# The S5 scan of a hybrid encoder as two real scans in a turning frame, with reordered mixer steps

## The chip, the cores and the metric

The kernel runs on one core of a Trainium2 chip. What counts is the device time of one execution, in microseconds (us). Engines are named as the profile names them: PE is TensorE (PEld its weight loads), DVE is VectorE, ACT is ScalarE, POOL is GpSimd, SP is SyncE, which issues DMA transfers. "PEclk" is the clock that TensorE was granted, as a share of full speed.

## The reference

Two layers over x of 512 tokens by 1024 channels. Each layer projects x once, and gives the columns to three mixers: a bidirectional S5 (256 channels), a bidirectional gated linear attention in chunks of 64 (256 channels), and a windowed attention with rotary embedding (512 channels). Then follow the output projection with a layer norm, and a feed-forward part of width 4096 (squared ReLU) with another.

```
lam_bar = exp(lam * step)                       # complex, per group and state
bu = einsum('zgph,blgh->zblgp', b_bar, u)
h[t] = lam_bar * h[t-1] + bu[t]                 # forward; and the same backward
y = Re(c0 . h_f) + Re(c1 . h_b) + d * u ;  z = gelu(y) ;  y_A = val * sigmoid(gate)
x = LN(alpha*x + concat(y_A, y_B, y_C) @ w_out)
x = LN(alpha*x + relu(x @ w_ff1)**2 @ w_ff2)
```

## The kernel before

**Matmuls.** Each large product is taken as three (low by high, high by low, high by high; `mm3`, L251 to L254). A weight unit (`wunit`) is loaded by SP into `raw`, copied by ACT into WA (high half, L221), and its low half is the difference that DVE (sometimes POOL) makes (L248). The first of the three matmuls needs the low half.

**S5.** The 512 tokens of a group are 64 chunks of 8. `tb_params` makes, on DVE, the complex powers of lam_bar (`powers`). `tables(l)` makes from them the tables of one layer: the products L541 to L564, transposes on TensorE (tile `wst`, L568), the in-chunk kernel (tile `lag`, L576 to L582), and it writes them to scratch in HBM (`scr_st`, `scr_out`, and 15 transfers `scr_lag`, L588 and L590, on SP). `s5_states` gives the contribution of each chunk, `M.Vs`: real and imaginary part, 16 groups, 64 chunks on 128 partitions (64 states forward, 64 backward). `s5_scan` turns this into the state before each chunk, `M.H`. It takes two levels: inside blocks of 8 chunks a complex step for j = 1 to 7 (L761 to L764, four DVE instructions each); over the 8 block ends six complex steps on 128x32 (L772 to L775); and a third part that adds the power times the block's entry state (L785 to L793), whose second half, the imaginary parts, is on POOL in layer 0 and on DVE in layer 1 (`sc1`). `s5_out` multiplies M.H with the output tables.

**Linear attention.** `gla_gates` (decays, L613, L615, tile `gs`), `gla_scores` (q_in L636, k_in, scores `gsc` L645 on TensorE, masked copy L646 on DVE), `gla_states`, `gla_out` (statistics in GLS), `gla_y` (`goT` on TensorE).

**Windowed attention.** Rotary embedding L873 to L875, queries transposed as `qT` (L907), split at L914 and L915, then `swa`.

**Feed-forward.** For some block pairs `ff1_pair` (L1036 on) takes a Strassen form: two weight blocks r1 and r2 are loaded by SP (L1041, L1042) into the scratch tile MA, alternately in its columns 0 to 2047 and 2048 to 4095; DVE makes sums (L230), ACT copies each unit into WA and DVE makes its low half (L1060); the products are the 128x256 tiles `f1s`.

**Order.** The steps of a mixer are written in the order that the table `seq` gives for each layer (`u` and `st0`/`st1` are the S5 input and states, `g0`, `g2`, `g3` the other projections, `w0` to `w3` the windowed attention of each query block, `y` the end of the linear attention). A scheduler then places every instruction by that order as priority, so the queues interleave the steps. Layer 1's tables are written behind the first quarter of layer 0's first feed-forward matrix (`tables(1)`, released by a step named `ff3`), and so run under the feed-forward stage. Scratch tiles are shared: MA holds attention scratch in the mixer, tables in front of layer 1, and the blocks r1 and r2.

Of the kernel before, what the change touches and what calls it, by code (L numbers as in the profile page):

```python
# [64 lines left out]
def trunk(tc, I, out, dbg=None):  # L65
# [300 lines left out]
    def tb_params():  # L366
# [116 lines left out]
        V.tensor_scalar(AIS_[:, 0], APW_[:, 1, :, 0], -1.0, None, op0=MUL)
        V.tensor_copy(AIS_[:, 1], APW_[:, 1, :, 0])
        V.tensor_scalar(A8S_[:, 0], APW_[:, 1, :, 7], -1.0, None, op0=MUL)
        V.tensor_copy(A8S_[:, 1], APW_[:, 1, :, 7])

# [261 lines left out]
    def s5_scan(l):  # L749
        APW, AIS, A8S = [t[:, :, 16 * l:16 * l + 16] for t in (APW_, AIS_, A8S_)]  # L750
        DB("V", M.Vs.rearrange("p r g b j -> p (r g b j)"))
        DB("APW", APW_.rearrange("p a b c -> p (a b c)"))
# [6 lines left out]
        for j in range(1, 8):
            x = M.Vs[:, :, :, :, j - 1]  # L760
            V.tensor_tensor(T1, x, ar, op=MUL)  # L761
            V.tensor_tensor(T2, x[:, ::-1], ai, op=MUL)
            V.tensor_tensor(T1, T1, T2, op=ADD)
            V.tensor_tensor(M.Vs[:, :, :, :, j], M.Vs[:, :, :, :, j], T1, op=ADD)  # L764
        a8 = bc(APW[:, 0, :, 7], 1, 2)
        V.memset(EST[:, :, :, 0], 0.0)
        for b in range(7):
            if b == 0:
                V.tensor_copy(EST[:, :, :, 1], M.Vs[:, :, :, 0, 7])
                continue  # L770
            x = EST[:, :, :, b]
            V.tensor_tensor(ETM[:, 0], x, a8, op=MUL)  # L772
            V.tensor_tensor(ETM[:, 1], x[:, ::-1], A8S, op=MUL)
            V.tensor_tensor(ETM[:, 0], ETM[:, 0], ETM[:, 1], op=ADD)
            V.tensor_tensor(EST[:, :, :, b + 1], M.Vs[:, :, :, b, 7], ETM[:, 0], op=ADD)  # L775
# [2 lines left out]
        for r, eng, n, buf in ((0, V, 8, y2), (1, E("sc1", l), 4, TAB[:, 512:1024])):
            for i in range(16 // n):
                gs = slice(n * i, n * i + n)  # L780
                P1 = buf[:, 0:64 * n].rearrange("p (g b j) -> p g b j", g=n, b=8)
# [561 lines left out]
```

## Time and profile before

| | us |
|---|---|
| median of three runs | 1242.35 (1240.74 to 1243.05) |
| the profiled execution | 1247.4 |
| its span in the trace | 1245.6, granted clock 0.977 |
| PE busy | 1169.3 (94%) |
| DVE busy | 901.5 (72%) |
| ACT busy | 553.4 (44%) |
| POOL busy | 164.1 (13%) |

The profile describes the one execution of 1247.4 us. A busy share is an average over stages; a stage's own limit is read from a window of it, and from what the engine with the gap waited for. Sections of the run: layer 0's mixer lasts to about 280 us, the output projection and the feed-forward part to about 640, layer 1's mixer to about 910, the rest is layer 1's projection and feed-forward.

### The profile page before, as it was taken

What the parts mean: (1) busy time and instruction counts of PE and PEld (TensorE: products, weight loads), DVE (VectorE), ACT (ScalarE), POOL (GpSimd) and SP (SyncE); (2) the same over time, 40 slices, a digit from 0 to 9 for tenths busy, and PEclk for the clock granted to TensorE, in tenths of its full rate; (3) what the DMA queues carried; (4) which work ended last, traced back from release to release, by engine and by line L of the source; (5) the groups of instructions that cost most, each with busy time, mean ns of one, the idle gap of its engine ahead of it and who ended that gap; (6) DMA issues with size and microseconds to landing.
All of it is one profiled execution on the core that took longest, in us unless ns stands there. A gap on an engine that the chain in (4) does not pass through costs nothing.

```text
span 1245.6 us, 18803 instructions
## 1 busy us (share of the span) xinstructions
PE 1169.3 (94%) x7400; PEld 985.5 (79%) x7400; DVE 901.5 (72%) x1727; ACT 553.4 (44%) x937; POOL 164.1 (13%) x123
## 2 busy tenths in 40 slices
PE   6696978999999999999999989799999999999997
PEld 4684765678888889989987867556898898998986
DVE  8986988659875675758564399883987485764957
ACT  4253247534522543725533535572465272461640
POOL 3422352112000000000141020220400000000000
PEclk9898999999999999999999999899999999999999
DMA  6340431113453532412422414302144142250331
GB/s 219 103 153 9 73 123 52 52 34 105 123 166 143 159 104 68 150 54 69 153 82 74 158 34 66 122 17 85 35 138 150 51 142 79 88 164 20 100 121 68
DMA packets 50616, 121.68 MB, mean 98 GB/s; under 512 B 13280, under 2 KB 20320, under 8 KB 50528
## 3 DMA queue, kind: packets, MB, share of 16 engines
q1 hardware_dynamic: 37680, 103.53, 25.2%
q10 hardware_dynamic: 12848, 16.95, 5.3%
q8 instruction: 58, 0.95, 0.3%
q14 instruction: 30, 0.25, 0.1%
HBM read 110.53 MB, written 8.88 MB: 96 GB/s over the span
## 4 chain that ended last, share of the span: by engine, by line
PE 67%; DVE 9%; DMA 2%; ACT 2%; issue 1%; SPq 1%; ACTq 0%; DVEq 0%
PE o L252 11%; PE o L253 11%; PE o L254 11%; PE f1s L252 6%; PE f1s L254 6%; PE f1s L253 6%; PE so L968 2%; PE proj L253 1%; PE proj L254 1%; PE proj L252 1%; PE f1e L253 1%; PE pT L962 1%; PE f1e L254 1%; PE f1e L252 1%; DVE XR L319 1%
## 5 line engine op out<-in xcount | busy, mean ns | idle before, releaser
L221 ACT ACTIVATE WA<-raw 128x1024 fp32r<-128x1024 f32 (+2 forms) x129 | 132.4, 1029 | 140.7 <-DMA raw<-in_w_ff 39.2
L248 DVE TENSOR_TENSOR WA<-raw,WA 128x1024 fp32r<-128x1024 f32 (+1 forms) x102 | 121.8, 1195 | 89.8 <-ACT WA L221 89.8
L221 ACT ACTIVATE WA<-MA 128x1024 fp32r<-128x1024 f32 (+1 forms) x72 | 64.5, 913 | 138.4 <-PE o L254 102.2
L979 DVE SCALAR_TENSOR_TENSOR XR<-XR,o 128x512 f32<-128x512 f32 (+1 forms) x81 | 52.7, 676 | 90.4 <-PE o L254 90.3
L1060 DVE TENSOR_TENSOR WA<-MA,WA 128x1024 fp32r<-128x1024 f32 (+1 forms) x72 | 74.4, 1043 | 17.0 <-ACT WA L221 17.0
L252 PE MATMUL f1s<-xs,WA 128*128 128x256 f32 x288 | 81.6, 283 | 0.2 <-DVE MA L230 0.2
L254 PE MATMUL f1s<-xs,WA 128*128 128x256 f32 x288 | 81.5, 283 | 0.0
L253 PE MATMUL f1s<-xs,WA 128*128 128x256 f32 x288 | 81.5, 283 | 0.0
L248 POOL TENSOR_TENSOR WA<-raw,WA 128x1024 fp32r<-128x1024 f32 (+2 forms) x27 | 61.4, 2280 | 130.0 <-ACT WA L221 123.6
L230 POOL TENSOR_TENSOR XR<-XR,lt 128x512 f32<-128x512 f32 (+1 forms) x13 | 18.5, 1421 | 394.1 <-ACT XR L218 394.1
L230 DVE TENSOR_TENSOR MA<-MA,f1s 128x256 f32<-128x256 f32 x120 | 49.6, 418 | 28.6 <-PE f1s L254 19.6
L252 PE MATMUL o<-WA,yYa 128*128 128x512 f32 (+1 forms) x162 | 64.0, 395 | 0.8 <-DVE XR L979 0.7
L253 PE MATMUL o<-WA,yQ 128*128 128x512 f32 (+1 forms) x164 | 63.4, 386 | 0.0
L252 PE MATMUL o<-WA,yQ 128*128 128x512 f32 (+1 forms) x164 | 63.3, 386 | 0.0
L252 PE MATMUL o<-WA,yYb 128*128 128x512 f32 (+1 forms) x162 | 63.0, 389 | 0.0
L253 PE MATMUL o<-WA,yYa 128*128 128x512 f32 (+1 forms) x162 | 63.0, 389 | 0.0
L253 PE MATMUL o<-WA,yYb 128*128 128x512 f32 (+1 forms) x162 | 63.0, 389 | 0.0
L254 PE MATMUL o<-WA,yYb 128*128 128x512 f32 (+1 forms) x162 | 62.8, 389 | 0.0
L252 PE MATMUL o<-WA,yP 128*128 128x512 f32 x160 | 62.8, 392 | 0.0
L254 PE MATMUL o<-WA,yYa 128*128 128x512 f32 (+1 forms) x162 | 62.7, 387 | 0.0
L254 PE MATMUL o<-WA,yQ 128*128 128x512 f32 (+1 forms) x164 | 62.7, 385 | 0.0
L253 PE MATMUL o<-WA,yP 128*128 128x512 f32 x160 | 62.7, 392 | 0.0
(460 smaller groups left out, 3566.0 us busy)
## 6 DMA issues: line engine op xcount, KB each, us to landing
raw<-in_w_ff SPq DMA_DIRECT2D x80, 512.0 KB, 3.5
MA<-in_w_ff SPq DMA_DIRECT2D x48, 512.0 KB, 3.5
raw<-in_wg SPq DMA_DIRECT2D x23, 512.0 KB, 4.0
raw<-in_w_out SPq DMA_DIRECT2D x16, 512.0 KB, 3.9
scr_out<-MA SPq DMA_DIRECT2D x8, 512.0 KB, 3.7
yc<-scr_out ACTq DMA_DIRECT2D x8, 512.0 KB, 4.4
raw<-in_wg SPq DMA_DIRECT2D x8, 288.0 KB, 2.9
MA<-in_s5cb ACTq DMA_DIRECT2D x8, 256.0 KB, 4.2
```

The costliest lines, as they stand in the source:

```text
L221: S.activation(out=o_, in_=i_, func=AF.Copy)
L230: eng.tensor_tensor(o_, a, b, op=op)
L248: (eng or V).tensor_tensor(WA[:, i, 1, c], raw[:, c], WAf[:, i, 0, c], op=SUB)
L252: T.matmul(ps, a[1], b[0], start=first, stop=False)
L253: T.matmul(ps, a[0], b[1], start=False, stop=False)
L254: T.matmul(ps, a[0], b[0], start=False, stop=last)
L319: V.scalar_tensor_tensor(x[:, c], x[:, c], mean, M.lng[:, c], op0=SUB, op1=MUL)
L962: T.transpose(ps[:, b * 128:b * 128 + 128], P[:, h, b * 128:b * 128 + 128], ident)
L968: T.matmul(ps[64 * v:64 * v + 64, :], av[:, tt - 1 + b0 + b, 64 * v:64 * v + 64], M.pT[v][:, b].rearrange("p h q -> p (h q)"), start=(b == ...
L979: V.scalar_tensor_tensor(x, x, scale, ps, op0=MUL, op1=ADD)
L1060: V.tensor_tensor(WA[:, u, 1, c], src, WAf[:, u, 0, c], op=SUB)
```

## The change

`s5_scan` no longer works in blocks. With lam_bar to the 8th written as a real size times a turn, every chunk's contribution is turned back by its chunk number (cos and sin in the new table ROT, 128 x 2 x 16 x 64), so that what remains is a recurrence with a real factor. That is one `tensor_tensor_scan` for the real and one for the imaginary parts (128x1024 each, the factor in TAB, set to 0 at each group's first chunk). Then the result is turned forward again, with the last sum written into M.H. All of it is on DVE, except the copy of the factor into TAB on ACT.

`tb_params` no longer makes the powers 1 to 8 of lam_bar to the 8th (APW and its copies); it squares the size and the turn three times (MG8, RW) and corrects the turn's length (`unit_`). `turns(l)` makes ROT from RW by doubling, six rounds of four DVE instructions, in two scratch areas of MA (columns 0 to 2047). `turns(0)` is a new step in layer 0 behind the gates, `turns(1)` is written behind `tables(1)`. The order table `seq` changes in both layers; in layer 0, `scan` comes behind `out`, `g2` ahead of the scores, `y` behind `w3`.

```diff
-    "seq": ["u st0 g0 tb st1 gates scan scores states sink g2 out g3 y keys late s5o w0 w1 w2 w3", "u tb st0 st1 g0 gates scan scores sink g2 states out g3 y keys late s5o w0 w2 w1 w3"],
+    "seq": ["u g0 st0 tb st1 gates turns g2 scores states sink out scan g3 keys late w0 s5o w3 y w1 w2", "tb g0 u gates st0 st1 scan scores states sink g2 out g3 y keys late s5o w0 w2 w1 w3"],
...
-        V.tensor_copy(APW_[:, :, :, 0], PW[:, :, :, 8])
-        powers(APW_, -1)
...
+        for k in range(3):
+            V.tensor_tensor(MG8, mag if k == 0 else MG8, mag if k == 0 else MG8, op=MUL)
+        wc, ws = RW[:, 0], RW[:, 1]
+        for k in range(3):
+            V.scalar_tensor_tensor(u1, ws, 2.0, wc, op0=MUL, op1=MUL)
+            V.tensor_tensor(u2, ws, ws, op=MUL)
+            V.tensor_scalar(wc, u2, -2.0, 1.0, op0=MUL, op1=ADD)
+            V.tensor_copy(ws, u1)
+        unit_(wc, ws)
...
+    def turns(l):
+
+        t = [MA[:, 1024 * i:1024 * i + 1024] for i in range(2)]
+        V.tensor_copy(ROT[:, :, :, 0], RW[:, :, 16 * l:16 * l + 16])
+        k = 1
+        while k < 64:
+            n = 32 * k
+            t1, t2 = [x[:, 0:n].rearrange("p (r g k) -> p r g k", r=2, g=16) for x in t]
+            x = ROT[:, :, :, 0:k]
+            wr, wi = [bc(bc(ROT[:, r, :, k - 1], 1, 2), 3, k) for r in range(2)]
+            V.tensor_tensor(t1, x, wr, op=MUL)
+            V.tensor_tensor(t2, x, wi, op=MUL)
+            V.tensor_tensor(ROT[:, 0, :, k:2 * k], t1[:, 0], t2[:, 1], op=SUB)
+            V.tensor_tensor(ROT[:, 1, :, k:2 * k], t1[:, 1], t2[:, 0], op=ADD)
+            k *= 2
+            if k == 8:
+                unit_(ROT[:, 0, :, 7], ROT[:, 1, :, 7])
...
     def s5_scan(l):
...
+        copyA(m3, bc(MG8[:, 16 * l:16 * l + 16], 2, 64))
+        V.memset(m3[:, :, 0], 0.0)
+        V.tensor_tensor(h, v, bc(co, 1, 2), op=MUL)
+        V.tensor_tensor(v, v, bc(si, 1, 2), op=MUL)
+        V.tensor_tensor(h[:, 0], h[:, 0], v[:, 1], op=ADD)
+        V.tensor_tensor(h[:, 1], h[:, 1], v[:, 0], op=SUB)
+        for r in range(2):
+            V.tensor_tensor_scan(v[:, r], TAB, h[:, r], 0.0, op0=MUL, op1=ADD)
+        x = [TAB, M.y2]
+        for r in range(2):
+            V.tensor_tensor(x[r], v[:, r], co, op=MUL)
+        V.tensor_tensor(v, v, bc(si, 1, 2), op=MUL)
...
+        for r in range(2):
+            for d in range(2):
+                pr = slice(64 * d, 64 * d + 64)
+                a, b = [y[pr].rearrange("p (g c) -> p g c", g=16)[:, :, 0:63] for y in (x[r], v[:, 1 - r])]
+                ho = M.H[pr, r, :, 1:64] if d == 0 else M.H[pr, r, :, 62::-1]
+                V.tensor_tensor(ho, a, b, op=ADD if r else SUB)
...
                 with tc.issue_after(state[CFG["tf"]].ins):
                     run(tables(1))
+                    turns(1)
```

Three places in the order of the instructions. Line numbers behind the change are a few lower or higher (the low half L248 is L246, the weight load L244 is L242, L541 to L546 are L572 to L577, L588 and L590 are L619 and L621, L636 is L667, L646 is L677, L1041 and L1042 are L1054 and L1055).

DVE at the start, where the parameters end and the first layer's tables begin, before (yc is scratch, PSR holds the powers, WA the weight halves):

```order
L454 TENSOR_TENSOR APW_75<-yc_104 128x32x4
L455 TENSOR_TENSOR yc_104<-APW_75 128x128
L456 TENSOR_TENSOR yc_104<-APW_75 128x128
L457 TENSOR_TENSOR APW_75<-yc_104 128x32x4
L485 TENSOR_SCALAR A8S_77<-APW_75 128x32
L486 COPY A8S_77<-APW_75 128x32
L541 TENSOR_TENSOR yc_104<-TAB_84,PSR_78 128x64
L542 TENSOR_TENSOR yc_104<-TAB_84,PSR_78 128x64
L543 TENSOR_TENSOR MB_69<-yc_104 128x64
L544 TENSOR_TENSOR yc_104<-TAB_84,PSR_78 128x64
L545 TENSOR_TENSOR yc_104<-TAB_84,PSR_78 128x64
L546 TENSOR_TENSOR MB_69<-yc_104 128x64
```

and now:

```order
L488 COPY RW_76<-yc_104 128x32
L577 TENSOR_TENSOR MB_69<-yc_104 128x64
L485 SCALAR_TENSOR_TENSOR yc_104<-RW_76 128x32
L486 TENSOR_TENSOR yc_104<-RW_76 128x32
L588 TENSOR_TENSOR yc_104<-PSR_78,MB_69 128x512
L487 TENSOR_SCALAR RW_76<-yc_104 128x32
L488 COPY RW_76<-yc_104 128x32
L246 TENSOR_TENSOR WA_66<-raw_574,WA_66 128x576
L494 TENSOR_TENSOR UNT_87<-RW_76 128x32
L495 TENSOR_TENSOR UNT_87<-RW_76 128x32
L587 TENSOR_TENSOR yc_104<-PSR_78,MB_69 128x512
L496 TENSOR_TENSOR UNT_87<-UNT_87 128x32
```

The first table products (L541, now L572) stood behind the whole power table; they now stand among the few small squarings, and the low half of the weight unit behind several of them.

SP under the first feed-forward quarter of layer 0, before (scr_lag1 is layer 1's scratch, MA the tile for r1 and r2):

```order
L572 DMA scr_out1_95<-MA_68 128x1024 x2
L1042 DMA MA_68<-in_w_ff1 128x1024
L1041 DMA MA_68<-in_w_ff1 128x1024 x3
L588 DMA scr_lag1_97<-MA_68 16x16x16 x2
L590 DMA scr_lag1_97<-MA_68 16x16x16
L588 DMA scr_lag1_97<-MA_68 16x16x16
L590 DMA scr_lag1_97<-MA_68 16x16x16
```

and now:

```order
L1054 DMA MA_68<-in_w_ff1 128x1024
L619 DMA scr_lag1_97<-MA_68 16x16x16 x2
L621 DMA scr_lag1_97<-MA_68 16x16x16
L619 DMA scr_lag1_97<-MA_68 16x16x16
...
L619 DMA scr_lag1_97<-MA_68 16x16x16
L621 DMA scr_lag1_97<-MA_68 16x16x16
L1054 DMA MA_68<-in_w_ff1 128x1024
L1055 DMA MA_68<-in_w_ff1 128x1024 x2
```

One load of a later pair still stands ahead of the 15 transfers; the loads of the first pair's r1 and r2, which stood ahead of them, now stand behind them (the row with L1054 is r1, the first of the two with L1055 is r2), and r1 also waits for the last instruction of `turns(1)`.

DVE in layer 1's mixer, where the queries of the linear attention are made (L636, now L667), before:

```order
L762 TENSOR_TENSOR yb_5508<-yc_5509,AIS_76 128x256
L763 TENSOR_TENSOR yb_5508<-yb_5508 128x256
L661 MEMSET ya_5507 128x64
L764 TENSOR_TENSOR yc_5509<-yc_5509,yb_5508 128x256
L761 TENSOR_TENSOR yb_5508<-yc_5509,APW_75 128x256
L762 TENSOR_TENSOR yb_5508<-yc_5509,AIS_76 128x256
L635 COPY DEC_86<-yb_5508 128x8
L636 SCALAR_TENSOR_TENSOR lt_5152<-hx_5506,yb_5508 128x512
L763 TENSOR_TENSOR yb_5508<-yb_5508 128x256
L230 TENSOR_TENSOR MA_68<-hx_5506,yb_5508 128x512
```

and now (L789 is the first product of the new scan):

```order
L666 COPY DEC_85<-yb_5495 128x8
L667 SCALAR_TENSOR_TENSOR lt_5139<-hx_5493,yb_5495 128x512
L228 TENSOR_TENSOR MA_68<-hx_5493,yb_5495 128x512
L223 COPY MB_69<-proj_6137 128x128
L886 TENSOR_TENSOR RT_86<-hx_5493,CS_70 128x64
L887 TENSOR_TENSOR RT_86<-hx_5493,CS_70 128x64
L888 TENSOR_TENSOR hx_5493<-RT_86 128x4x16
L896 SCALAR_TENSOR_TENSOR MB_69<-MB_69,proj_6137 128x256
L789 TENSOR_TENSOR yc_5496<-yc_5496,ROT_75 128x2048
L677 COPY_PREDICATED MA_68<-CI_72,gsc_5930 128x512
```

The query product stood behind most of the scan's block steps; it now stands ahead of the scan.

## Rows read from the trace of the kernel before

**Rows 1.** The page, part 1: busy us (share of the span) and instructions.

```profile
PE 1169.3 (94%) x7400; PEld 985.5 (79%) x7400; DVE 901.5 (72%) x1727; ACT 553.4 (44%) x937; POOL 164.1 (13%) x123
```

**Rows 2.** Windows by stage: us, busy per engine (instructions), clock, DMA share, GB/s.

```profile
0.00:280.00 280.00, 235.95 (x1559) 178.59 (x1560) 224.60 (x542) 121.01 (x255) 86.68 (x74) 0.94 0.30 91
420.00:640.00 220.00, 219.71 (x1356) 198.06 (x1355) 143.77 (x220) 99.09 (x134) 10.25 (x5) 1.00 0.34 112
640.00:910.00 270.00, 249.05 (x1622) 194.32 (x1621) 194.13 (x430) 127.62 (x258) 55.18 (x37) 0.96 0.24 70
```

**Rows 3.** Windows inside layer 1's mixer.

```profile
710.00:730.00 20.00, 14.01 (x160) 11.62 (x158) 16.65 (x31) 10.64 (x17) 5.32 (x4) 1.00 0.10 37
730.00:780.00 50.00, 48.37 (x342) 35.86 (x342) 48.87 (x132) 22.18 (x36) 6.43 (x5) 0.97 0.36 74
780.00:810.00 30.00, 21.52 (x176) 16.74 (x175) 25.84 (x72) 17.74 (x50) 6.24 (x6) 0.83 0.30 107
```

**Rows 4.** Windows inside layer 0's mixer.

```profile
100.00:130.00 30.00, 22.07 (x229) 15.67 (x229) 19.20 (x37) 6.54 (x14) 7.34 (x6) 0.77 0.08 9
180.00:200.00 20.00, 13.58 (x130) 11.34 (x124) 17.67 (x42) 10.38 (x25) 5.03 (x4) 0.83 0.42 139
```

**Rows 5.** What PE waited for, 700 to 840: total us, times, longest.

```profile
PE gsc L645 <- ACT MA L221: 5.2, 1, 5.2
PE goT L711 <- POOL ya L230: 3.7, 1, 3.7
```

**Rows 6.** What PE waited for, 30 to 64.

```profile
PE proj L253 <- DVE WA L248: 4.5, 1, 4.5
PE wst L568 <- DVE MA L558: 3.9, 1, 3.9
```

**Rows 7.** What PE waited for, 180 to 200.

```profile
PE qT L907 <- DVE GLS L295: 3.4, 1, 3.4
```

**Rows 8.** DVE by form, 715 to 795: count, busy us, mean ns, idle before.

```profile
L764 DVE TENSOR_TENSOR yc<-yc,yb 128x256 f32<-128x256 f32 x7 | 5.5, 782 | 0.1
...
L761 DVE TENSOR_TENSOR yb<-yc,APW 128x256 f32<-128x256 f32 x7 | 4.4, 626 | 0.1
...
L793 DVE TENSOR_TENSOR yc<-yc,TAB 64x252 f32<-64x252 f32 x8 | 3.3, 414 | 0.1
...
L793 DVE TENSOR_TENSOR yc<-yc,yb 64x504 f32<-64x504 f32 x4 | 2.7, 675 | 0.0
...
L775 DVE TENSOR_TENSOR TAB<-yc,ETM 128x32 f32<-128x32 f32 x6 | 2.2, 366 | 0.1
...
L615 DVE TENSOR_TENSOR ya<-ya 128x1024 f32<-128x1024 f32 x1 | 1.2, 1226 | 2.4 <-ACT ya L218 2.4
```

**Rows 9.** DVE by form, 130 to 180.

```profile
L786 DVE TENSOR_TENSOR yb<-APW,TAB 128x512 f32<-128x512 f32 x2 | 2.2, 1104 | 0.0
```

**Rows 10.** Timeline of DVE, 36 to 64: start us, us, instruction.

```profile
37.08 1.10 DVE L481 COPY APW<-yc 128x64 f32<-128x64 f32 x1
...
53.90 1.30 DVE L486 COPY A8S<-APW 128x32 f32<-128x32 f32 x1
```

**Rows 11.** Timeline of DVE, 722 to 733 us.

```profile
727.14 0.69 DVE L636 SCALAR_TENSOR_TENSOR lt<-hx,yb 128x512 f32<-128x512 f32 x1
```

**Rows 12.** Timeline of all engines, 405 to 419 us.

```profile
405.35 1.06 ACT L221 ACTIVATE WA<-MA 128x1024 fp32r<-128x1024 f32 x1 [3.21 <-DMA MA<-in_w_ff]
...
407.11 1.22 DVE L1060 TENSOR_TENSOR WA<-MA,WA 128x1024 fp32r<-128x1024 f32 x1
...
409.50 0.82 SPq L588 DMA_DIRECT2D scr_lag<-MA  x2
...
417.52 0.45 SPq L590 DMA_DIRECT2D scr_lag<-MA  x1
...
418.53 0.28 PE L253 MATMUL f1s<-XTQ,WA 128*128 128x256 f32 x1
```

**Rows 13.** The loads of r1 (L1041): us from issue to landing.

```profile
DMA to landing us min/median/max: 3.3/3.5/6.1
```

More of the change, by code (lines that the diff above doesn't have):

```diff
@@ L111, in trunk @@
     RT = sb.tile([128, 2, 128], F32, name="RT")
+    UNT = sb.tile([128, 2, 32], F32, name="UNT")
     KON = sb.tile([128, 4], F32, name="KON")
@@ L427, in tb_params @@
         V.tensor_scalar(e1, e1, -2.0, 1.0, op0=MUL, op1=ADD)
+        V.tensor_copy(RW[:, 0], e1)
+        V.tensor_scalar(RW[:, 1], e3, 2.0, None, op0=MUL)
         V.memset(PW[:, 0, :, 0], 1.0)
@@ L479, in tb_params, with unit_ @@
         V.tensor_tensor(ri, ri, e4, op=MUL)
-        V.tensor_copy(APW_[:, :, :, 0], PW[:, :, :, 8])
-        powers(APW_, -1)
[L483 to L486, printed above, removed]
+        for k in range(3):
[7 more added lines that the diff above has]
+        unit_(wc, ws)
+    def unit_(c, s_):
+        u1, u2 = UNT[:, 0, 0:c.shape[-1]], UNT[:, 1, 0:c.shape[-1]]
+        V.tensor_tensor(u1, c, c, op=MUL)
+        V.tensor_tensor(u2, s_, s_, op=MUL)
+        V.tensor_tensor(u1, u1, u2, op=ADD)
+        V.tensor_scalar(u1, u1, -0.5, 1.5, op0=MUL, op1=ADD)
+        V.tensor_tensor(c, c, u1, op=MUL)
+        V.tensor_tensor(s_, s_, u1, op=MUL)
+    def turns(l):
[14 more added lines that the diff above has]
+                unit_(ROT[:, 0, :, 7], ROT[:, 1, :, 7])
     def tables(l):
@@ L759, in s5_scan @@
[L759 to L775, printed above, removed]
+        v = M.Vs.rearrange("p r g b j -> p r (g b j)")
@@ new lines, in s5_scan @@
+        h = M.H.rearrange("p r g c -> p r (g c)")
+        co, si = [ROT[:, r].rearrange("p g c -> p (g c)") for r in range(2)]
+        m3 = TAB.rearrange("p (g c) -> p g c", g=16)
+        copyA(m3, bc(MG8[:, 16 * l:16 * l + 16], 2, 64))
[4 more added lines that the diff above has]
+        V.tensor_tensor(h[:, 1], h[:, 1], v[:, 0], op=SUB)
@@ L776, in s5_scan @@
+        for r in range(2):
[4 more added lines that the diff above has]
+        V.tensor_tensor(v, v, bc(si, 1, 2), op=MUL)
         V.memset(M.H[0:64, :, :, 0], 0.0)
         V.memset(M.H[64:128, :, :, 63], 0.0)
[L778 to L781, printed above, removed]
-                P2 = buf[:, 64 * n:128 * n].rearrange("p (g b j) -> p g b j", g=n, b=8)
-                Ar, Ai = bc(APW[:, 0, gs], 2, 8), bc(APW[:, 1, gs], 2, 8)
-                Er, Ei = bc(EST[:, 0, gs], 3, 8), bc(EST[:, 1, gs], 3, 8)
-                eng.tensor_tensor(P1, Ar, Er if r == 0 else Ei, op=MUL)
-                eng.tensor_tensor(P2, Ai, Ei if r == 0 else Er, op=MUL)
-                eng.tensor_tensor(P1, P1, P2, op=SUB if r == 0 else ADD)
-                for d in range(2):
-                    pr = slice(64 * d, 64 * d + 64)
-                    pf = P1[pr].rearrange("p g b j -> p g (b j)")[:, :, 0:63]
-                    vf = M.Vs[pr, r, gs].rearrange("p g b j -> p g (b j)")[:, :, 0:63]
-                    ho = M.H[pr, r, gs, 1:64] if d == 0 else M.H[pr, r, gs, 62::-1]
-                    eng.tensor_tensor(ho, vf, pf, op=ADD)
@@ L1201, in trunk @@
                  "g0": lambda: run(proj(I["wg0"][l], 288, evac_g0, "g1")), "gates": lambda: gla_gates(l),
-                 "scan": lambda: s5_scan(l), "scores": lambda: gla_scores(l), "states": lambda: gla_states(l),
+                 "scan": lambda: s5_scan(l), "turns": lambda: l or turns(0), "scores": lambda: gla_scores(l), "states": lambda: gla_states(l),
                  "sink": sink, "g2": lambda: run(proj(I["wg2"][l], 512, evac_g2, "g2")), "out": lambda: gla_out(l),
```

17 lines of the change are left out of this document (3 added, 14 removed).

## The prediction

> **What bounds the kernel now.** First the busy times [rows 1]: TensorE is busy for 1169.3 of 1245.6 us, so at most 76 us can come from filling its gaps, and the change takes no matmul away. Then the same by stage [rows 2]: in 420 to 640 us (feed-forward) TensorE has no gap at all, 219.71 of 220 us, with VectorE (DVE) at 65%; in the mixer of layer 0 it lacks 44 us, in that of layer 1 21 us. Inside the second mixer [rows 3] DVE is busy 48.87 of 50 us between 730 and 780, while TensorE loses 6.0 us before it, 1.6 in it and 8.5 behind it, and runs at a granted clock of 0.83 from 780 to 810. In the first mixer [rows 4] TensorE lacks 7.9 us in 100 to 130, where DVE has 10.8 us free, and 6.4 us in 180 to 200, where DVE is at 88%. The list of what TensorE waited for names the work: in layer 1 the scores `gsc`, 5.2 us [rows 5]; at the start the transposed tables `wst`, 3.9 us [rows 6]; in layer 0 `qT` behind the statistics of the linear attention, 3.4 us [rows 7]. All three are DVE queues. So the change is worth what a shorter or reordered DVE queue gives in the mixers, less what it costs in the feed-forward stage, which has no gap to hide a wait.
>
> **The scan.** The old one in layer 1 is, on DVE, 28 instructions of L761 to L764 at about 0.65 us (the rows give 0.63 and 0.78), 24 of L772 to L775 at about 0.24, 6 of 128x512 at 0.69 (as L636 of that size, [rows 11]), 12 of 128x256 at 0.41, and the sums of L793, 4 at 0.675 and 8 at 0.414 [rows 8]: 18.2 + 5.8 + 4.1 + 4.9 + 6.0 = 39.0 us. In layer 0 the 128x256 half of the end (12 + 8 instructions) is on GpSimd, so DVE has about 28 us, and 3 us more because its instructions beside GpSimd's stretch: L786 (128x512) takes 1.10 us there [rows 9] instead of 0.69. The new one has no row for its 128x2048 products. The rows 0.69 (512 wide) and 1.23 (1024 wide, L615) [rows 8, 11] rise 0.54 per 512, so 2048 is 2.3 us: 3 x 2.3 + 4 x 1.23 + 4 sums of 64x1008 at 1.22 + 0.3 of memsets = 17.0 us. For the scan instruction no row exists: at least one pass, 1.23, at most two dependent ones, 2.46; I take one pass, nearest in operands and size to L615, so 17.0 + 2.5 = 19.5 us a layer, or 22 at the other end. The table copy (128x1024) goes to ScalarE, which is 44% busy. DVE is relieved of 19.5 us in layer 1 (17 at the other bound) and 11 in layer 0.
>
> [...]
>
> **The turn tables.** Each `turns` issues, besides a copy, 6 rounds of four products and sums, two of 32k and two of 16k elements for k = 1 to 32: 6048 elements at 1.05 ns (0.54 us per 512) and 24 starts of 0.15 us (0.69 less 512 elements) make 10, and the six small ones of `unit_` at about 0.2 one more: 11 us. `turns(0)` stands behind the first layer's gates, where DVE has 10.8 us free [rows 4]. I cost it at nothing; if the hole does not cover it, half of it, 5 us, comes back. `turns(1)` is dealt with below.
>
> **The parameter tables at the start.** The power table of the old scan is removed: 29 instructions between L481 at 37.08 and L486 at 53.90 us [rows 10], many of them stretched like these two to over 1 us: of the 18.1 us to the end of the last, some 3 are other work, so about 15 us go. 23 small ones take their place (some 5 us). The table products that `wst` waits for come some 10 us of queue earlier. Not more than the wait of 3.9 us [rows 6] and the 4.5 us behind the weight half in the same rows can go, and that half now stands seven places further back, behind part of the tables. I take 3 us, between 0 and 6.
>
> **Layer 0's mixer.** The gaps of 100 to 130 hang on `wst`, `gsc` and chains through other engines and stay largely; those of 180 to 200 hang on a DVE queue that is 11 us shorter. GpSimd's part of the scan goes too, and with it the stretch. Of 6.4 us idle and 2.3 us of lower clock (0.17 of 13.6) [rows 4], I take 6; between 0 and 12, the upper end with 5 us from the first hole.
>
> **Layer 1's mixer.** Before, `q_in` (L636) starts at 727.14 [rows 11], behind fourteen instructions of the scan, and `gsc`, which needs it, waits 5.2 us [rows 5]. After, it stands ahead of the whole scan, whose first instruction comes seven DVE rows behind it; so those 5.2 us go. Later the masked copies of the second direction stand behind L798 (2.3 us) and four sums of 1.22: `gsc`'s buffers are freed up to 7 us late, which gives most of that back there. From then on DVE is some 18 us ahead and the 8.5 us at 780 to 810 with the clock beside them (0.17 of 21.5, 3.7 us) go in part. 5.2 + 12 - 8 = 9 us; between 4 and 16, which is all the idle time in [rows 3].
>
> **The first pair of feed-forward, layer 0.** This is the part that gives back. `turns(1)` uses the first 2048 columns of MA as scratch: there the pair's blocks r1 and r2 are loaded. Before, they were issued ahead of the 15 `scr_lag` transfers that SP sends from 409.50 to 417.52, and the first low half was made at 407.11 [rows 12]: 11 us before TensorE came to it at 418.53. After, r1 waits for the last instruction of `turns(1)`, which can begin only when the `lag` products have read MA (about 402) and needs 11 us and the 2 to 3 us of other work put between; so the two loads are issued behind all of `scr_lag`, at about 418. They land 3.5 us later in the median, 3.3 to 6.1 at the ends [rows 13], about 4 with three together; then the copy on ScalarE, 1.06, and the low half on DVE, 1.22 [rows 12]. 418 + 4 + 1.06 + 1.22 = 424.3: TensorE waits about 6 us, DVE's next sums stand in the same queue (1 us), and the clock falls after such a gap: 0.97 over 50 us behind the 5.2 us of `gsc` [rows 3], 1.5 us. Together some 8 us; between 3 (issued at 416, since one transfer in that queue took 1.7 us instead of 0.5, and landing in 3.3) and 11 (landing in 6.1).
>
> **Sum.** -3 - 6 - 9 + 8 = -10 us on the profiled execution of 1247.4 us, 1237.4. That execution lies 5.05 us above the median of the three runs, 1242.35, so I forecast 1232.3.
>
> **Rivals.**
> A second way is full relief: the start gives 6, layer 0 12, layer 1 16, and the pair's loads cost 6. -28, so 1214. For it: DVE saturated in front of both late gaps. Against: the masked copies behind 2.3-us instructions, and in layer 0 the wait for other engines.
> The slower side: the r1 and r2 loads decide alone. If they land at 423 and the stall with its clock costs 11 us, the change is slower from the point at which the mixers give less than 8.5; with 3 us from them (the order of the attention's chain on TensorE and not DVE's busy time holds the rest) it is 1250. For it: no gap in 420 to 640 [rows 2] and a queue that is seen to be occupied until 417.97. Against: it needs three terms at their low ends.
> No change: the scan is shorter but its long instructions hold back the attention (`gsc` buffers again, 7 us), layer 1 gives 5, layer 0 with the start 3, the pair takes 8: 1242.
> A fourth comes from GpSimd. L786 at 1.10 us beside it and 0.69 without [rows 9, 11] shows that DVE and GpSimd hold each other up; an instruction of 2.3 us then holds a GpSimd sum that long. Layer 1's `goT` waited 3.7 us for such a sum [rows 5]; 2.3 us more there and half as much at two others would leave 1237. [...]
>
> **How the numbers follow.** The forecast with its terms between their ends, and the GpSimd case within it, 0.57: 1223 to 1240. Full relief 0.19: 1211 to 1223. No change 0.11: 1239 to 1245. Slower 0.13: above 1245. About 0.2% (2.5 us) is what a measurement of this kernel can tell from no change. Faster gets the forecast's 0.57 nearly whole, relief's 0.19 and a little of the third: 0.77; same 0.09; slower 0.14. A range for 8 in 10 leaves out the lower half of relief and two thirds of the slower case: 1216 to 1247.
>
> **What would show it.** Right: no wait of `gsc` near 724 and DVE no longer full from 760 on; scan instructions of 1.2 to 2.5 us; at about 418 a gap of 5 to 7 us ahead of the first `f1s` matmul, released by DVE's low half with a load behind it; `wst` without its 3.9 us. Wrong: r1 and r2 issued before the `scr_lag` transfers or no gap at 418, which takes 8 off; or `gsc` stalls as long as before with a scan behind it, which takes 5 to 9 of gain away.

## The result, and the profile after

The changed kernel takes 1257.18 us (median of 4, 1256.65 to 1258.77); the kernel before took 1242.7 beside it. Ratio 1.0114, interval 1.0085 to 1.0142: slower by 14 us, where 10 us of gain were forecast. The profiled execution has a span of 1255.0 us.

Busy times after, the answer to [rows 1]:

```profile
PE 1182.3 (94%) x7400; PEld 985.4 (79%) x7400; DVE 888.9 (71%) x1663; ACT 558.8 (45%) x939; POOL 150.4 (12%) x103
```

VectorE does 12.6 us less, as the change intends. But TensorE, with the same 7400 records, is busy 13 us *more*. Of the forecast's cost terms only the 1.5 us of lower clock at the first pair lengthens busy time.

The stages no longer lie at the same times, so [rows 2 to 4] are best answered by windows between the same events: start to the first `f1e` matmul of layer 0 (projections and mixer), from there to layer 1's first `proj`, to its first `gsc`, to its first output projection `o`. Before (columns as in [rows 2]: us, busy of PE, PEld, DVE, ACT, POOL, granted clock, DMA share, GB/s):

```profile
0.00:290.26 290.26, 246.21 (x1608) 187.08 (x1609) 234.62 (x558) 125.73 (x262) 93.23 (x77) 0.94 0.31 92
290.26:652.52 362.26, 360.03 (x2186) 318.23 (x2184) 253.00 (x404) 155.92 (x220) 20.85 (x12) 1.00 0.35 115
652.52:730.49 77.97, 69.34 (x539) 59.43 (x536) 38.67 (x70) 35.58 (x65) 12.43 (x9) 0.98 0.30 96
730.49:837.53 107.04, 96.57 (x654) 67.65 (x655) 97.39 (x254) 59.93 (x142) 18.75 (x15) 0.94 0.27 70
```

and after:

```profile
0.00:290.95 290.95, 250.43 (x1609) 189.38 (x1609) 226.51 (x533) 128.30 (x263) 77.20 (x57) 0.93 0.29 91
290.95:662.90 371.95, 365.19 (x2186) 319.56 (x2184) 262.20 (x435) 156.13 (x220) 20.91 (x12) 0.99 0.34 112
662.90:735.63 72.73, 70.78 (x521) 59.91 (x519) 29.59 (x54) 36.44 (x66) 13.07 (x10) 1.00 0.32 102
735.63:846.45 110.82, 97.56 (x673) 66.14 (x673) 92.95 (x199) 62.10 (x142) 20.43 (x14) 0.94 0.25 67
```

Layer 0 up to its feed-forward part: +0.7 us (forecast -9). The feed-forward part: +9.7 (forecast +8), of which 5.2 are longer busy time of the same 2186 records (the 2.6 of lower clock shown below among them). Layer 1 to its scores: -5.2, and then +3.8: -1.5 together (forecast -9). Some 18 matmuls have moved from the first of these two stretches to the second, so the sum is what counts. Behind that the two differ by less than 1 us. Each table is one execution; the first stretch takes 287.0 and 289.6 us in e14 and e15 below, which have the instructions of the kernel before, so a difference there is known to some 3 us.

The forecast stall at the first pair is there. Timeline after, 405 to 427 us (start, us, engine, line, instruction, and what ended the wait before it):

```profile
414.35 0.69 DVE L514 TENSOR_TENSOR ROT<-MA 128x512 f32<-128x512 f32 x1
...
417.88 0.38 SPq L1054 DMA_DIRECT2D MA<-in_w_ff  x1
...
418.30 1.23 SPq L1055 DMA_DIRECT2D MA<-in_w_ff  x2
...
422.21 1.06 ACT L219 ACTIVATE WA<-MA 128x1024 fp32r<-128x1024 f32 x1 [1.51 <-DMA MA<-in_w_ff]
...
424.20 1.22 DVE L1073 TENSOR_TENSOR WA<-MA,WA 128x1024 fp32r<-128x1024 f32 x1
...
425.48 0.58 PE L250 MATMUL f1s<-XTQ,WA 128*128 128x256 f32 x1 [5.41 <-DVE WA L1073]
```

The last instruction of `turns(1)`, the two loads issued behind all `scr_lag` transfers (before: ahead of them, [rows 12]), the copy, the low half, and TensorE 5.41 us late. The clock falls behind it (the column behind POOL's busy time):

```profile
425.00:430.00 5.00, 4.53 (x21) 4.53 (x22) 5.00 (x8) 2.62 (x4) 0.00 (x0) 0.50 0.25 82
430.00:435.00 5.00, 5.00 (x42) 5.00 (x42) 4.23 (x7) 2.56 (x4) 0.00 (x0) 0.94 0.78 255
```

At 0.50 the 4.53 us of busy time do half as much (21 matmuls, 42 in the next window's 5.00): 2.3 us, and 0.3 in the next window. 5.41 + 2.6 = 8.0.

The scan on DVE, layer 1, by form (count, busy us, mean ns):

```profile
L794 DVE TENSOR_TENSOR_SCAN yc<-TAB,yc 128x1024 f32<-128x1024 f32 x2 | 4.5, 2287 | 0.0
...
L806 DVE TENSOR_TENSOR yc<-TAB,yc 64x1008 f32<-64x1008 f32 x2 | 2.4, 1198 | 0.0
L790 DVE TENSOR_TENSOR yc<-yc,ROT 128x2048 f32<-128x2048 f32 x1 | 2.3, 2294 | 0.0
```

What TensorE waited for in layer 1, 700 to 840 us, the answer to [rows 5]:

```profile
PE zT L853 <- DVE SM__80 L961: 3.0, 1, 3.0
PE sc L946 <- ACT MA L216: 2.9, 4, 1.6
PE proj L250 <- DVE MB L896: 2.2, 1, 2.2
PE qT L920 <- DVE MA L888: 1.3, 1, 1.3
```

The 5.2 us of `gsc` are gone, and so is the wait of `goT`. Others have come: `zT` (the transposes of the S5 output) stands behind a small instruction of the softmax on VectorE, `sc` (the scores of the windowed attention) behind the exponentials. The gap late in this mixer is still there, with the lower clock (window as in [rows 3], where 780 to 810 lacks 8.5 us at 0.83):

```profile
790.00:810.00 20.00, 13.13 (x132) 9.87 (x129) 17.44 (x61) 11.24 (x30) 3.86 (x4) 0.82 0.22 71
```

At the start, 30 to 64 us, the answer to [rows 6]: `wst` 1.8 us less, the weight half 0.7 more, so 1.1 us where 3 were forecast.

```profile
PE proj L251 <- DVE WA L246: 5.2, 1, 5.2
PE wst L599 <- DVE MA L593: 2.1, 1, 2.1
```

And one wait in layer 0 that the forecast does not have. Timeline after, 143 to 165 us (GLG is the row of gains of the linear attention's norm; its load at 147.59 is layer 1's):

```profile
144.21 0.42 DVE L228 TENSOR_TENSOR MB<-MB,GLG 128x256 f32<-128x256 f32 x1
144.30 1.92 ACTq L818 DMA_DIRECT2D hx<-scr_lag  x4
146.78 0.34 ACTq L823 DMA_DIRECT2D yc<-scr_out  x1
147.59 0.36 ACTq L627 DMA_DIRECT2D GLG<-in_gla_ln_g  x1
...
153.60 0.29 DVE L628 TENSOR_SCALAR GLG<-GLG 128x256 f32<-128x256 f32 x1 [7.46 <-DMA GLG<-in_gla_ln_g]
153.81 1.33 DVE L677 COPY_PREDICATED MA<-CI,gsc 128x512 f32<-128x512 uint8 x2
...
154.58 2.08 PE L676 MATMUL gsc<-MA 128*128 128x512 f32 x2 [3.39 <-DVE MA L677]
```

The load may go out only when layer 0's row has had its last reader (144.21 to 144.63), and it stands in ScalarE's queue of transfers, behind the loads of the S5 output (`hx`, `yc`): it goes out 3 us after that reader. VectorE, which is to halve the new row, stands there from 146.14 on for 7.46 us, with layer 0's masks queued behind. Before, the load went out at 147.24, right behind the last reader, and landed at nearly the same time, but VectorE came to it at 150.83 (timeline before):

```profile
152.82 0.35 DVE L597 TENSOR_SCALAR GLG<-GLG 128x256 f32<-128x256 f32 x1 [1.99 <-DMA GLG<-in_gla_ln_g]
```

### The profile page after: what moved, and what is told of

The parts are those of the page before. It is cut to its first block, busy times and chain, and to the rows that moved or that the text cites. A ratio compares the mean times of both kernels' runs of the same rounds, so it can differ in the third digit from the quotient of the medians.

```text
span 1255.0 us, 18704 instructions
## 1 busy us (share of the span) xinstructions
PE 1182.3 (94%) x7400; PEld 985.4 (79%) x7400; DVE 888.9 (71%) x1663; ACT 558.8 (45%) x939; POOL 150.4 (12%) x103
## 4 chain that ended last, share of the span: by engine, by line
PE 75%; DVE 16%; DMA 3%; ACT 2%; issue 2%; SPq 1%; ACTq 0%; POOL 0%; DVEq 0%
PE o L250 12%; PE o L251 11%; PE o L252 11%; PE f1s L250 6%; PE f1s L251 6%; PE f1s L252 6%; PE so L981 2%; PE proj L250 2%; PE proj L251 2%; PE proj L252 2%; PE pT L975 1%; PE f1e L251 1%; PE f1e L252 1%; PE f1e L250 1%; PE f L250 1%
## 5 line engine op out<-in xcount | busy, mean ns | idle before, releaser
L246 DVE TENSOR_TENSOR WA<-raw,WA 128x1024 fp32r<-128x1024 f32 (+1 forms) x102 | 121.9, 1195 | 86.3 <-ACT WA L219 83.8
L246 POOL TENSOR_TENSOR WA<-raw,WA 128x1024 fp32r<-128x1024 f32 (+2 forms) x27 | 62.0, 2301 | 173.0 <-ACT WA L219 162.1
```

What stands on the lines that cost most here:

```text
L246: (eng or V).tensor_tensor(WA[:, i, 1, c], raw[:, c], WAf[:, i, 0, c], op=SUB)
```

## The experiments

Ratios are to the kernel before on the same chip in the same runs. The changed kernel run once more with e5 to e7 (`c_after`) gave 1.012, 1.0091 to 1.0149.

### The first pair of the feed-forward part

**e1**: `turns(1)` with other scratch.

```diff
-        t = [MA[:, 1024 * i:1024 * i + 1024] for i in range(2)]
+        t = [(M.lt if l else MA)[:, 1024 * i:1024 * i + 1024] for i in range(2)]
```

> The changed kernel, with one edit: layer 1's turn table is built in the idle tile lt instead of columns 0 to 2047 of MA, so the loads of the first feed-forward pair (r1, r2) wait for no turn table. Theory 1 (the buffer makes the gap of 5.4 us ahead of the first f1s matmul, with 2.6 us of lower clock behind it): the gap is gone, and the time is 8 to 10 us below the changed kernel's 1257, about 1248. Rival (the 11 us of DVE work in that stretch make it, wherever their scratch lies): the gap stays within 2 us and the time within 3 us of 1257.

Measured 1262.2 us, 1.0149 [1.0127, 1.0171], and the stall is longer (timeline):

```profile
419.80 2.20 SPq L1054 DMA_DIRECT2D MA<-in_w_ff  x2
...
428.32 0.58 PE L250 MATMUL f1s<-XTQ,WA 128*128 128x256 f32 x1 [7.60 <-DVE WA L1073]
```

Missed. Free of MA, the turns were placed ahead of layer 1's tables on VectorE (326 to 358 us), so the tables came late, and the loads wait for the last reader of the tables in MA (a `lag` product on TensorE). The loads do not hang on the scratch alone but on whatever of VectorE's work stands ahead of the last use of MA.

**e5**: `turns(1)` behind the whole first feed-forward block instead.

```diff
-                    turns(1)
+            if l == 0 and c == 3:
+                turns(1)
```

> The changed kernel, with one edit: layer 1's turn table is built behind the last quarter of layer 0's first feed-forward matrix and no longer behind layer 1's tables, with the same scratch in MA. Nothing of it stands ahead of the first pair's loads of r1 and r2, neither as a buffer nor in DVE's queue. Theory 1 (work put between the last lag product and the pair, or ahead of it, makes the gap, in MA or in the queue alike): no gap ahead of the first f1s matmul, feed-forward part of layer 0 back to 362 us from 372, time 8 to 10 us below the changed kernel's, some 1248. Rival (the gap comes from something else in the reordered kernel): the gap stays, time within 3 us of the changed kernel.

Measured 1254.06 us, 1.009 [1.0066, 1.0115]; the loads stand ahead of `scr_lag` again and the stall of `f1s` is gone. The feed-forward stage takes 367.8 us instead of 371.8 in `c_after`. So of the 14 us this term is 3 to 4, less than the 8 us seen at the place. Part of the difference is seen: with the stall gone, TensorE waits 1.0 us for the sums of that pair (`f1s` behind MA) and 0.8 for `o`, waits that the changed kernel does not have. What is left of that stage's loss is not idle time. The 8 to 10 us expected were missed.

### The scan and the order

**e4**: before, with the scan left out (the chunks' contributions are copied into M.H as they are).

```diff
-        for j in range(1, 8):
...
+                V.tensor_copy(ho, vf)
```

> The kernel before in its old order, with the work of the scan left out in both layers: the states are only copied into place, so DVE has some 60 us less and GpSimd 20 instructions less. It bounds what any faster scan can give. If DVE's queue bounds the mixers (my prediction): 18 to 30 us faster than before, 1212 to 1225. If the gaps hang on chains through other engines: at most 8 us faster, 1234 or more.

Measured 1238.9 us, 0.9954 [0.9923, 0.9984]: 2 to 10 us in all, against 15 forecast for the two mixers. The total hides two opposite things. Windows (start to first `f1e`; layer 1's two stretches), and the wait at the first pair of layer 1's feed-forward part, 0.6 us before:

```profile
0.00:277.99 277.99, 244.72 (x1608) 186.15 (x1609) 209.10 (x498) 125.87 (x262) 74.51 (x57) 0.94 0.32 95
...
640.82:714.44 73.62, 67.75 (x540) 58.30 (x538) 29.99 (x56) 35.45 (x65) 12.63 (x9) 1.00 0.39 123
714.44:822.44 108.00, 94.82 (x652) 66.77 (x652) 77.47 (x187) 59.53 (x141) 19.71 (x15) 0.97 0.23 54
```

```profile
PE f1s L252 <- DVE WA L1031: 3.9, 1, 3.9
```

Layer 0 up to its feed-forward part is 12.3 us shorter (290.3 to 278.0): there VectorE's queue does hold TensorE. In layer 1, VectorE is relieved of 28.6 us (136.1 to 107.5) and the two stretches are only 3.4 us shorter (185.0 to 181.6): a shorter queue of VectorE does not shorten that mixer. Behind layer 1's mixer 3.8 us are lost again, with the new stall at a place that the edit does not touch. So the total is no strict ceiling of what a faster scan can give.

**e7**: after, without the scan and both turns.

```diff
-            V.tensor_tensor_scan(v[:, r], TAB, h[:, r], 0.0, op0=MUL, op1=ADD)
...
-                V.tensor_tensor(ho, a, b, op=ADD if r else SUB)
+                V.tensor_copy(ho, a)
```

> The changed kernel with the work of the scan and both turn tables left out; the states are only copied into place. It bounds what the new scan costs in the new order. Theory B (the scan is not on the path, the order of the steps and the chains set the mixers): within 5 us of the run with the late turn table. If DVE's queue bounds the mixers: 15 us or more below it.

Measured 1252.91 us, 1.0085 [1.0061, 1.011]: with *no* scan at all the changed kernel is still slower than before, and within 1.2 us of e5, which has it. The total again hides a balance. Up to the first `f1e`, e7 is 7.4 us shorter than e5 (283.7 to 291.1; the 5.1 us in which e5's scores wait for the masks are gone), and the feed-forward part is 2.0 shorter. Layer 1's mixer is 2.4 us longer and the rest 5.4, where the first pair stalls as in e4:

```profile
PE f1s L250 <- DVE WA L1059: 3.8, 1, 3.8
```

So the scan and the turns do cost time in layer 0. That the sum comes out equal does not show that they are free; in layer 1's mixer they are not what costs.

**e3**: before with the new order alone (old scan).

```diff
-    "seq": ["u st0 g0 tb st1 gates scan scores states sink g2 out g3 y keys late s5o w0 w1 w2 w3", ...
+    "seq": ["u g0 st0 tb st1 gates g2 scores states sink out scan g3 keys late w0 s5o w3 y w1 w2", ...
```

> The kernel before with its old scan, and only the new order of the mixer steps. Theory A (the order costs): 5 to 10 us slower than before, 1247 to 1253. Theory B (the order is neutral, the relief is unusable): within 3 us of before.

Measured 1264.8 us (the median of 1256.7, 1264.8 and 1269.3), 1.0161 [1.0111, 1.0211]: some 20 us, between 14 and 26, more than either theory. Layer 1 from scores to output projection takes 128.9 us instead of 107.0, with this wait of TensorE the longest from 640 to 880:

```profile
PE sy L821 <- DMA yc<-scr_out: 6.0, 1, 6.0
```

**e2**: e1 with the old order, the new scan right behind the turns; **e10**: the same on e9 (below).

> As the run before it (scratch in lt), and the order of the mixer steps of the kernel before in both layers, with the turn table of layer 0 right ahead of the scan. Theory A (the new scan relieves DVE as worked out, and the new order of the steps takes it back): 5 to 10 us faster than the run with the scratch alone, 1238 to 1243 or less. Theory B (the relief of DVE does not reach TensorE, whatever the order): within 3 us of that run.

> As the run before it (late turn table of layer 1, ROT behind the x tiles), with the order of the mixer steps of the kernel before. It tells what the new order is worth with the new scan, at one placement. If the new order costs as it does with the old scan (20 us): 1230 or less. If the new scan needs its new order: 5 to 12 us above the run before it, 1248 to 1256.

Measured 1.0239 [1.0214, 1.0263] against e1's 1.0149, and 1.013 [1.01, 1.0159] against e9's 1.004: the new scan is 11 to 12 us worse in the old order of both layers. Neither theory of e2 came. Scan and order belong together, and in these runs neither alone is a gain; with the new scan, the order in layer 1 alone makes no difference (e17 below).

**e6**: e5 with the scan in two halves of 8 groups, to let the masks in between.

```diff
+        hs = [slice(0, 512), slice(512, 1024)]
+        for q in hs:
+            V.tensor_tensor(h[:, :, q], v[:, :, q], bc(co[:, q], 1, 2), op=MUL)
...
```

> As the run before it, with the new scan cut into two halves by groups: its instructions of 2.3 and 1.2 us become twice as many of about 1.2 and 0.65 us, some 3 us more of DVE work a layer. Theory C (the mixers' gain is lost because masked copies and PSUM evacuations stand behind long DVE instructions): the waits of TensorE for the masked copy and for the rotary evacuation shrink, and the time falls 3 to 8 us below the run before it. Theory B (the gaps hang on chains through other engines, and DVE's scan is not on the path): within 2 us of it, or slower by the 3 us of added work.

Measured 1261.5 us, 1.0149 [1.0122, 1.0176], 7 us over e5, more than either theory allowed. Shorter instructions gain nothing here; why the halves cost 7 us was not settled.

### The places of the tiles

The new tables take 8832 bytes per partition (ROT, RW, MG8, UNT), the old ones took 2816 (APW, AIS, A8S, ETM). So all work tiles allocated behind them (lt, hx, ya, yb and the three x tiles) lie 6016 bytes = 47 x 128 further; WA, allocated ahead, stays. **e8** does only this to the kernel before; its instructions are the same in the same order.

```diff
+    PAD = sb.tile([128, 1504], F32, name="PAD")
```

> The kernel before, with an unused tile of 6016 bytes per partition added (and one memset of one column) so that all tiles behind it, the x halves XT and the hidden tiles among them, lie at the addresses that they have in the changed kernel. Every engine has the same instructions in the same order. The profile of the changed kernel shows 128x512 matmuls at a spacing of 0.2325 us, before 0.2278, whatever the stage. Theory D (the place of the operands in SBUF sets that spacing): 0.2325 here too, some 2400 matmuls by 0.0047, so 9 to 12 us slower than before, 1252 to 1255. Rival (the spacing comes from the order or the other engines' work in the changed kernel): 0.2278 and within 2 us of before.

Measured 1250.24 us, 1.0048 [1.0031, 1.0065], and

```profile
PE 1176.2 (94%) x7400; PEld 982.7 (78%) x7400; DVE 903.8 (72%) x1728; ACT 552.7 (44%) x937; POOL 164.2 (13%) x123
```

6.9 us more busy time of TensorE than in [rows 1], from an unused tile. In time it is some 6 us, half of what was expected: the 128x512 matmuls have the longer spacing (232.4 ns start to start on `yP`, before 227.4), but the 128x256 matmuls of the Strassen products follow each other sooner (118.7 ns in the changed kernel, whose work tiles lie as in e8, before 119.9). **e9** is e5 with ROT behind the x tiles and a pad of 128 bytes, so that the work tiles lie 2048 bytes nearer to WA than before.

> The changed kernel with the late turn table of layer 1, and the table ROT placed behind the x tiles, with a pad of 128 bytes: the x and hidden tiles lie 2048 bytes below their place in the kernel before. Instructions and their order are those of the run with the late turn table. Theory D: spacing back to 0.2278 and 9 to 12 us faster than the run with the late turn table, 1242 to 1246, level with before. Rival: no change from 1254.

Measured 1250.21 us, 1.004 [1.0021, 1.0058], e5 had 1.009: some 6 us, not the 9 to 12 expected, and not level with before. Its feed-forward stage is as before, busy for 360.27 us (e5: 364.63, both 2186 records):

```profile
292.53:655.54 363.01, 360.27 (x2186) 318.17 (x2184) 260.51 (x434) 156.67 (x220) 20.80 (x12) 1.00 0.35 115
```

**e11**, **e14**, **e15**: before, with 128 bytes between WA and the work tiles, with 256, and with 128 ahead of all tiles (WA and the others move together); one execution each.

> The kernel before with an unused tile of 128 bytes instead of 6016. It tells which part of the address matters: 6016 is 128 over a multiple of 256, and 384 over one of 512. If it is the place within 256 bytes, the spacing is 0.2325 here as well; if a coarser one, 0.2278.

> The kernel before with 256 unused bytes per partition between the small tables and the work tiles (128 bytes in e11). Theory D1 (what counts is whether the tiles that the weights in WA are multiplied with lie an odd or an even number of 128-byte steps further than before): start to start of 128x512 matmuls as before, 0.227 to 0.229 us, time within 0.3% of before. Rival D2 (any shift costs, or the finer address counts): 0.232 to 0.233 us as in e8 and e11, 0.4 to 0.6% more.

> The kernel before with 128 unused bytes per partition ahead of all its tiles, so that WA and the tiles multiplied with it move together. Theory R (the distance between the two operands counts): 0.227 to 0.229 us between 128x512 matmuls, as before. Rival A (the address itself counts): 0.232 to 0.233 us, and 0.4 to 0.6% more time.

Measured 1252.48, 1245.12 and 1247.35 us, the kernel before 1245.3 beside e11 and 1244.85 beside the others. The view of the tile `yP` shows it best: 160 matmuls of 128x512 on each of three lines, shortest/median/longest in ns. The first lines, of before, e8, e11, e14 and e15 in turn:

```profile
L252 PE MATMUL o<-WA,yP x160: 387/389/477, 242.4 to 651.5; 128*128 128x512 f32 x160
```

```profile
L254 PE MATMUL o<-WA,yP x160: 387/393/483, 242.2 to 654.9; 128*128 128x512 f32 x160
```

```profile
L254 PE MATMUL o<-WA,yP x160: 387/393/482, 240.1 to 653.7; 128*128 128x512 f32 x160
```

```profile
L254 PE MATMUL o<-WA,yP x160: 387/389/477, 239.2 to 648.7; 128*128 128x512 f32 x160
```

```profile
L254 PE MATMUL o<-WA,yP x160: 387/389/477, 241.8 to 651.0; 128*128 128x512 f32 x160
```

One matmul overlaps the next; from start to start, averaged over some 420 neighbours on `yP`, it is 227.4 ns before, 232.4 (e8), 232.6 (e11), 232.5 (after), 227.4 (e14 and e15), 227.5 (e9). Moving the two operands against each other by 1 or 47 steps of 128 bytes costs 5 ns, by 2 or 16 steps nothing, and moving both by one step nothing. Tiles `yQ`, `yYa`, `yYb`, `proj` and `f` show the same two levels: 227.0 to 228.2 ns before, 232.2 to 232.6 after.

### The row of gains in VectorE's queue

**e12**: e9 with one instruction on another engine; **e13**: the same on the kernel before.

```diff
-        V.tensor_scalar(GLG, GLG, 0.5, None, op0=MUL)
+        (G if l else V).tensor_scalar(GLG, GLG, 0.5, None, op0=MUL)
```

> e9 with one instruction on another engine: the halving of layer 1's row of gains (GLG, 256 numbers) goes from VectorE's queue to GpSimd's. In e9 VectorE stood idle 9.9 us before it, until the row's load had landed (issued at 148.2, landed 7.6 us later; the load waits for the last reader of layer 0's row), and four masks of the scores stood behind it, for the first of which TensorE waited 7.3 us. Theory G (a load of the next layer's row, waited for in VectorE's queue, is what layer 0's mixer lost): the 7.3 us wait of gsc is gone, first scores of layer 0 to first ff1 goes from 182.4 to 174 to 178 us, and the time falls by 4 to 8 us, to 1243 to 1246 (0.998 to 1.001 of before). Rival H (VectorE had slack there; the next thing, scores or a transposed tile, is late anyway): under 2 us, ratio 1.003 to 1.004.

> The kernel before with the same one instruction moved to GpSimd. VectorE waited 2.0 us for the row there and TensorE 1.3 us for the masks behind it. Theory G: 0 to 2 us less, ratio 0.998 to 1.000. Rival: GpSimd holds back its own splits behind the load, 0 to 2 us more.

Measured e12 1243.13 us, 0.9988 [0.9977, 1.0]; e13 1.0002 [0.9992, 1.0013]. In e9 the wait was 9.9 us, with `gsc` 7.3 late. In e12 (timeline) GpSimd waits for the row, and the masks (L678) do not:

```profile
148.32 1.60 DVE L678 COPY_PREDICATED MA<-CI,gsc 128x512 f32<-128x512 uint8 x2 [1.73 <-PE gsc L677]
148.54 0.36 ACTq L628 DMA_DIRECT2D GLG<-in_gla_ln_g  x1
...
156.39 0.85 POOL L629 TENSOR_SCALAR GLG<-GLG 128x256 f32<-128x256 f32 x1 [20.64 <-DMA GLG<-in_gla_ln_g]
```

Its windows (start to first `f1e`, feed-forward, layer 1's two stretches):

```profile
0.00:282.75 282.75, 245.05 (x1608) 186.07 (x1609) 226.69 (x534) 128.14 (x263) 77.39 (x58) 0.94 0.32 94
282.75:645.82 363.07, 360.10 (x2186) 318.15 (x2184) 260.47 (x434) 156.36 (x220) 20.81 (x12) 1.00 0.34 115
645.82:719.60 73.78, 71.69 (x522) 60.96 (x520) 29.63 (x54) 36.31 (x66) 13.09 (x10) 0.98 0.32 100
719.60:832.81 113.21, 96.40 (x673) 65.16 (x673) 92.75 (x199) 61.93 (x142) 20.57 (x14) 0.94 0.26 66
```

Layer 0 up to its feed-forward part is 7.5 us shorter than before (9.8 shorter than in e9), layer 1 is 2 us longer than before.

**e16**: e12 with layer 0's turns ahead of the gates, scratch in ya; **e17**: e12 with the old order in layer 1.

> e12 with layer 0's table of turns built earlier: its step ahead of the gates instead of behind them, its two halves of scratch in ya, which nothing uses until the gates, instead of MA, whose lag matrices TensorE still reads until 94 us. In e12 24 of its instructions stand on VectorE from 101 to 112 us, right ahead of the scan, and VectorE is busy without a gap from there to 140. Theory T (the table holds up the scan and the masks of layer 0): start to first ff1 2 to 6 us shorter than e12, ratio to before 0.994 to 0.997. Rival L (VectorE is as full from 60 to 80 us, where the table's instructions now stand between the lag products that TensorE waits for): start 2 to 5 us longer, ratio 1.001 to 1.004.

> e12 with the order of mixer steps of the kernel before in layer 1 alone, the new one kept in layer 0. The forecast was a gain of 9 us in layer 1's mixer; from its first projection to its first ff1 the kernel before takes 239.0 us, e10 (old order, new scan) 240.2, e12 (new order, new scan) 240.9. Theory N (in layer 1 the scan is not on the path in either order): the same within 2 us, ratio 0.997 to 1.000. Rival (layer 1 needs the new order for the new scan, as the two layers together did in e10): 3 to 8 us more, ratio 1.002 to 1.006.

Measured 1.006 [1.0039, 1.0081] and 0.9995 [0.9981, 1.0009]. In e16 the rival came true in kind, and more strongly: the first stretch is 11 us longer than in e12 (293.9 to 282.8), where 2 to 5 were expected. The turns stand between the products that TensorE waits for (`wst` waits 7.6 us from 40 to 130, 4.9 in e12), and the scores of layer 0 begin 6.4 us later than in e12. In e17 layer 1 takes the same within 1 us in either order (187.2, in e12 187.0). No version that computes the whole was measurably faster than the kernel before.

## Why the prediction was wrong

The account, in ratios: after 1.012, without the stall at the pair 1.009 (e5), with the tiles in their old relation to WA 1.004 (e9), with the gain row out of VectorE's queue 0.9988 (e12). About 4 + 6 + 6.5 us, each known to some 3 us. These three make the change slower. They do not make up the whole miss: without the pair's 8 us the forecast stood at -18, and e12 gains 1.5 (0 to 3). Most of the rest is layer 1.

**The scan's size.** Near, and at the upper end of its range. For layer 1, 39.0 and 19.5 us were worked out (22 at the other end); the rows of its lines give 39.6 and 21.3, mostly because of the scan instruction, taken at 1.23 us and measured at 2.29; a product of the same size takes 1.22 (L797 in layer 0). In layer 0, 39.0 less the twenty instructions on GpSimd is 30.8, not the 28 written; the rows give 31.7 and 22.2, so VectorE is relieved of 9.4 us there (forecast 11). The turns, taken at 11 us, add up to 11.3 in layer 0.

**The pair.** Right in mechanism and size at the place (5.41 + 2.6 = 8.0, forecast 8 from 6 + 1 + 1.5). Taking it away returned only some 4 us in the time; 1.8 us of other waits came in its place (e5), and where the rest goes was not settled.

**The start and layer 0.** Forecast -9, came +0.7. The mechanism was there: with one instruction moved (e12) it is -7.5, and without any scan (e4) -12.3. What failed is the step that read layer 0's gaps only by what ended them before. VectorE came 4.7 us earlier to a row that landed no earlier (153.6 against 152.8), so its 1.99 us of wait became 7.46. The forecast asked for each stall that goes what is late next on TensorE, but not what VectorE itself would run into when it comes early.

**Layer 1.** Forecast -9, came -1.5 in this run and +2 in e12. The first term, 5.2 us of `gsc`, came (the row names ScalarE's copy as what ended that wait; it copies what VectorE makes). The second failed: "from then on DVE is some 18 us ahead and the 8.5 us at 780 to 810 with the clock beside them (0.17 of 21.5, 3.7 us) go in part". The sum puts 12 there, which is not a part but the whole. e4 shows the premise wrong: with no scan at all this layer is only 3.4 us shorter. That VectorE was busy 48.87 of 50 us [rows 3] in front of those gaps was read as their cause. They were `goT` behind a sum on GpSimd [rows 5] and two waits for VectorE:

```profile
PE sy L819 <- DVE GLS L292: 2.6, 1, 2.6
PE pT L962 <- DVE yYa L718: 2.1, 1, 2.1
```

After the change these three are gone, but `zT`, `sc`, `proj` and `qT` wait 10.6 us in their place; e4 has yet others (`qT` 4.3, `so` 2.5, `sc` 2.4). So a wait that goes is replaced by another. The likely reason, not tested, is that the steps of these mixers hang on each other in chains through TensorE, VectorE and ScalarE. The third term, 8 us given back by late masks, shows no wait either: the last eight scores come 5.7 us later, counted from the layer's first `proj`, but TensorE has other work meanwhile.

**The order** as a whole was costed nowhere, only the place of `q_in` in layer 1. e10 and e3 show that it is worth 11 us with the new scan and costs some 20 with the old one.

**What no term held.** The matmuls' spacing, some 6 us: nothing in the diff names a matmul, but it resizes tables that lie ahead of the operands. "The feed-forward stage has no gap to hide a wait" was read; that it consists of nothing but matmuls, and so pays for each nanosecond of their spacing, was not.

**The rivals.** The slower side was to be decided by the pair's loads alone. They were one of three causes. Its condition, that the mixers give little, came true. The GpSimd case did not cost what it was priced at: a product of 0.73 us on GpSimd takes 2.82 beside the first product of layer 1's scan, one of 2.29 us on VectorE (at 736.6 and 736.5), but TensorE waits for GpSimd 1.8 us in all (before 6.0), and `goT` shows no wait.

## What to carry to other kernels

Before a queue is made shorter, list the instructions in it that wait for a transfer, and what the transfer itself waits for: an engine that comes early only waits longer there (here 7.46 us instead of 1.99), with all that stands behind it. To find what a faster step can be worth, leave the step out, and compare stage by stage, since a new stall elsewhere can hide the gain in the total. A busy engine ahead of a gap is not yet its cause. When a change resizes a table, compare the addresses of all tiles allocated behind it, and the busy time of the engine whose work did not change.

## What the runs showed of the hardware

In this kernel 128x512 matmuls (fp32r, each with its own weight load) follow each other at 227 to 229 ns where the two operands' tiles lie as before or are moved against each other by 2 or 16 steps of 128 bytes, and at 232 to 233 ns for 1 or 47. Over the kernel that is 0.5% (e8 against before, e5 against e9). In these runs the two levels go with the operands' distance: 128 bytes between the two gave 232.6 ns on `yP` (e11), 128 bytes ahead of both 227.4 (e15). What makes the two levels was not settled. The 128x256 matmuls moved less and not in the same way: 119.9 ns before, 118.7 in the changed kernel (+6016 bytes).

VectorE's scan over 128x1024 takes 2.29 us, 1.9 times a product of that size (1.22).
